# Attention stage of a streaming encoder: first loads ahead of the gates' weights, key stores on GpSimd, two tile pools, sample rows in two runs, cache keys in a value buffer

## The chip, the core and the metric

The kernel runs on one core of a Trainium2 chip. A core has five engines with a queue of instructions each: TensorE (PE, matrix products; its weight loads are shown as PEld), VectorE (DVE), ScalarE (ACT), GpSimd (POOL) and SyncE (SP), which here only issues transfers (DMAs). ACT and POOL issue transfers too. The metric is the device time in microseconds of one execution; the time given for a kernel is the median of its runs.

## The reference

One layer of a trunk, for a prompt of 2048 frames and a sample of 32 new frames, at model width 1024. After a normalisation and modulation by a condition vector, one input projection feeds two branches. Branch A is attention with 8 heads of 64, in chunks of 64 frames: each chunk sees itself and the 8 chunks before it, and the sample sees 512 cached rows and its own 32. Branch B is a gated linear recurrence. Sigmoid gates merge both, an output projection follows, and then a gated MLP with a convolution of width 3. For the attention of the sample:

```python
kk = jnp.concatenate([k_cache, k_new], axis=1)
vv = jnp.concatenate([v_cache, v_new], axis=1)
s = jnp.einsum('bqhd,bkhd->bhqk', q, kk).astype(jnp.float32) * (d ** -0.5) + bias
p = jax.nn.softmax(s, axis=-1).astype(vv.dtype)
o = jnp.einsum('bhqk,bkhd->bqhd', p, vv)
```

Everything is fp32. Products are made of high and low parts (`h`, `l` at the end of a name): a value is rounded by ACT to its high part, DVE subtracts for the low part, and PE makes two or three passes.

## The kernel before, in words

All 2080 columns (prompt and sample) stand transposed, in blocks of 416. The program has these stretches: preparation and the first input projections (to about 480 us); the recurrence of branch B, in chunks, with the projections to attention queries and keys (`qk_stream`) between its steps; the attention stage (from about 767 to 1486 us); then the merge and the MLP.

**Stores before the attention.** `t_evac` (L197) takes a block of a projection out of PSUM. For queries and keys it splits the block into a high part `qh` (ACT) and a low part `ql` (DVE) and stores both to DRAM (`qs`, `ks`): the high one by ACT's queue, the low one by SP's (L209 to L211), in two transfers of 64 rows each. The last chunk of the stream is the keys of heads 6 and 7 (`k`, c = 3), in five blocks. For the newest keys ACT also stores plain rows (`kr`, L216). The state of the recurrence is stored by POOL (`state_io`, L779).

**The attention stage** has 72 units: 8 heads by 9, where g = 0 to 7 are 256 query rows of the prompt each (two row blocks) and g = 8 is the 32 sample rows. A unit (L937) goes in steps: its loads (bias `nb` and the keys and values of chunk 0 in unit 0; queries `q2`; every second unit 512 more keys and values), its scores and softmax for the two row blocks, and then, for each block of 128 keys, a transpose of the probabilities `P` on PE, a copy out of PSUM and products with the values into `py`. The softmax goes through four engines: PE writes scores to `F` (far) and `PN` (near), DVE adds the bias and takes maxima into `mx`, ACT takes the exponentials (L927, L930), and POOL scales `P` by the reciprocal of the sum (L934).

Between these steps PE works through `filler`: the projections to the 2048 gate columns (16 chunks of 128 columns, five blocks of 416 each, eight slices of three passes: L78 to L80), whose weights come in pieces `wr` (L185) that ACT and DVE split into `wh` and `wl`, and then a projection of branch B. The loop from L1185 on sets how many filler steps stand between the steps of a unit and when the next unit's scores and the loads of the one after it come. Ahead of the loop stand the first loads, 16 steps of filler, and the first scores (L1173 to L1175). PE's order is this written order; in the attention stage a scheduler orders the other engines.

For the sample (g = 8, L995 to L1010) there are five blocks of keys: four of the cache, one of the new keys. For each block PE makes one transpose into a PSUM tile of its own, DVE copies it to `pt`, and PE makes one product with 64 value columns (L993), two blocks later; after each of the first steps a filler step may stand. The cached keys come as `ck` (L862), in a buffer of the ring of `P`, and are split into the key buffers by a deferred function (`LATE`).

Transfers issued by SP and ACT in the attention stage run over eight lanes that both queues share: before a transfer is issued, the one before it in its lane has to have landed. This is in the waits of the built program.

Of the kernel before, what the change touches and what calls it, by code (L numbers as in the profile page):

```python
# [21 lines left out]
TP, TS = 2048, 32  # L22
# [36 lines left out]
def encoder_step(ctx: ExitStack, tc: tile.TileContext, I, O):  # L59
# [116 lines left out]
    psm = pool(mix, "psm", bufs=2, space=PSUM)  # L176

    def w_pieces(wp, c0, n, w, kp, wr=2):

        hi = wp.tile([128, KD, w], F32R, name="wh", tag="wh")  # L180
        lo = wp.tile([128, KD, w], F32R, name="wl", tag="wl")

        def piece(kk):
            raw = wp.tile([128, kp, w], F32, name="wr", tag="wr", bufs=wr)
            nc.sync.dma_start(raw[:, :, :n], dap(w_in, kk * 128 * WIN + c0, [[WIN, 128], [128 * WIN, kp], [1, n]]))  # L185
            nc.scalar.activation(hi[:, kk:kk + kp, :n], raw[:, :, :n], AF.Copy)
            nc.vector.tensor_sub(lo[:, kk:kk + kp, :n], raw[:, :, :n], f32(hi[:, kk:kk + kp, :n]))

        return (hi, lo), [lambda kk=kk: piece(kk) for kk in range(0, KD, kp)]
# [7 lines left out]
    def t_evac(stg, kind, c, b, p):  # L197

        cols = slice(NB * b, NB * b + NB)
        if kind in "qk":  # L200
# [7 lines left out]
            dst = qs if kind == "q" else ks  # L208
            for x, r0, q_ in ((qh, 0, nc.scalar), (ql, 64, nc.sync)):  # L209
                for j in range(2):  # L210
                    q_.dma_start(dst[2 * c + j, r0:r0 + 64, cols], f32(x[64 * j:64 * j + 64]))  # L211
# [621 lines left out]
    with ExitStack() as st:  # L833
        stg = pool(st, "stgT", bufs=3)
        att_st = st.enter_context(ExitStack())
        at_ = pool(att_st, "att")
        psN = pool(att_st, "psN", space=PSUM)
# [10 lines left out]
        def load_chunk(h, c):  # L848
# [12 lines left out]
            if c == 5:  # L861
                ck = at_.tile([128, 512], F32, name="ck", tag="P", bufs=4)  # L862
                for r in (0, 64):
# [3 lines left out]
            else:  # L867
# [5 lines left out]
                else:  # L873
                    nc.sync.dma_start(vr, dap(vn, 512 * c * NCOL + 128 * pair, [[NCOL, 128], [128 * NCOL, 4], [1, 128]]))
            KH[c], KL[c] = kh, kl
            vr = vr[:, :, 64 * j:64 * j + 64]
            vs = None
            if c < 4:
# [6 lines left out]
                LATE.append(values)  # L885
            V[c] = (vr, vs)

# [5 lines left out]
        def scores(h, i, q2, qc, keys, PN):  # L893
# [20 lines left out]
            assert a == tot  # L914
            mx = at_.tile([128, 8], F32, name="mx", tag="mx", bufs=4)
            P = at_.tile([128, 640], F32, name="P", tag="P", bufs=4)
            nr = P[:m, far:tot]
# [19 lines left out]
        def unit(h, g):  # L937
# [57 lines left out]
            if g == 8:  # L995
                for x, kt in enumerate(steps):
                    first, last = x == 0, x == len(steps) - 1
                    pp_ = psP.tile([128, 2, 128], F32, name="pp", tag="pP")
                    kn = 128 if kt < 4 else TS
                    nc.tensor.transpose(pp_[:kn, 0, :TS], P[:TS, 128 * kt:128 * kt + kn], ident[:TS, :TS])  # L1000
                    pt = at_.tile([128, 128], F32, name="pt", tag="pt", bufs=3)
                    nc.vector.tensor_copy(pt[:kn, :TS], pp_[:kn, 0, :TS])
                    todo.append((py[0:64, :TS], vt[kt], pt[:kn, :TS], first, last))
                    if len(todo) > 2:
                        pv(1)
                    yield 1
                while len(todo) > 1:
                    pv(1)
                    yield 1
                pv(1)  # L1010
            else:
# [38 lines left out]
            if g == 8:  # L1050
                nc.vector.tensor_copy(ya[:, :TS], py[0:64, :TS])
                nc.sync.dma_start(yaT[64 * h:64 * h + 64, TP:T], ya[:, :TS])
# [119 lines left out]

        ustep(us[0])  # L1173
        pull(filler, 16)
        ustep(us[0])  # L1175
# [1155 lines left out]
```

## Time and profile before

| what | value |
|---|---|
| median of 3 runs | 3178.28 us (3174.66 to 3178.77) |
| the profiled execution | 3174.99 us, with a span of 3173.3 us |
| mean granted PE clock | 0.992 |
| PE busy | 3056.5 us, 96% of the span |
| DVE, ACT, POOL busy | 2243.6, 1649.5, 263.7 us |
| PE's longest idle time at the start of the attention | 5.86 us, ending at 782.46 |

In the rows of a timeline the first number is the start in us from the span's begin, the second the length in us; then come engine, line, operation, output and inputs with partitions x elements; `xN` means N instructions in a row; in brackets stands the idle time ahead of it and what ended it. `SPq` and `ACTq` rows are the issue of transfers by those queues. In a row of grouped instructions three times are minimum, median and maximum in ns. The granted clock is the share of full speed that PE got.

### The profile page before, as it was taken

The page shows a single profiled execution, that of the slowest core. Times are in us where ns is not written, and L with a number is a line of the kernel's source. Part 1 is how long each engine was busy: PE and PEld are TensorE (multiplying, and loading weights), DVE is VectorE, ACT ScalarE, POOL GpSimd, SP SyncE. Part 2 cuts the span into 40 slices and gives each one's busy share as a digit, 9 for nine tenths or more (in the row PEclk, how much of TensorE's full clock was granted, in tenths as well). Part 3 has the DMA queues.
Part 4 walks back from the last instruction along what each step waited for, and adds up shares of the span by engine and source line. Part 5 has one row for each costly group of instructions (what it writes and reads, how often), then busy time and mean ns, then how long its engine had stood idle before and what let it go on. Part 6 is the DMA issues. An engine that isn't in the chain of part 4 may idle for free. (4 is left out here: it accounts for less than half of the span.)

```text
span 3173.3 us, 56451 instructions
## 1 busy us (share of the span) xinstructions
PE 3056.5 (96%) x19748; PEld 2942.5 (93%) x19748; DVE 2243.6 (71%) x4903; ACT 1649.5 (52%) x3792; POOL 263.7 (8%) x417
## 2 busy tenths in 40 slices
PE   6999999999999999999999999999999999999997
PEld 4899999998999999988999899999999999999997
DVE  6735617774555545566577799998888778897877
ACT  4412224443554545544454655567656556576755
POOL 3201201111111111111000000000000000000001
PEclk9999999999999999999999999999999999999998
DMA  7344435554433333576457686787887667888784
GB/s 226 101 141 127 143 98 143 132 134 132 119 103 110 99 105 117 164 224 194 129 176 223 211 260 208 224 258 227 248 262 218 189 189 231 263 252 280 239 266 148
DMA packets 598799, 580.13 MB, mean 183 GB/s; under 512 B 53201, under 2 KB 527010, under 8 KB 598514
## 3 DMA queue, kind: packets, MB, share of 16 engines
q1 hardware_dynamic: 553826, 528.92, 55.6%
q10 hardware_dynamic: 44432, 47.34, 4.6%
q8 instruction: 155, 2.54, 0.3%
q14 instruction: 130, 1.06, 0.1%
q0 software_dynamic: 256, 0.26, 0.0%
HBM read 388.71 MB, written 187.65 MB: 182 GB/s over the span
## 5 line engine op out<-in xcount | busy, mean ns | idle before, releaser
L1876 PE MATMUL ad<-hA,hB 128*128 128x350 f32 (+2 forms) x1734 | 300.8, 323 | 5.3 <-DVE hB L1818 2.7
L78 PE MATMUL pm<-hA,wh 128*128 128x416 f32 x768 | 290.3, 378 | 0.0
L1876 PEld LDWEIGHTS ad<-hA,hB 128*128 128x128 f32 x1734 | 281.7, 189 | 7.3 <-ACT work L2002 3.8
L79 PE MATMUL pm<-hA,wh 128*128 128x416 f32 x768 | 269.9, 351 | 0.0
L80 PE MATMUL pm<-hA,wl 128*128 128x416 f32 x768 | 269.9, 351 | 0.0
L1818 DVE TENSOR_TENSOR hA<-raws,hA 128x512 fp32r<-128x512 f32 (+1 forms) x367 | 242.0, 668 | 12.5 <-ACT hA L1813 12.2
L1813 ACT ACTIVATE hA<-raws 128x512 fp32r<-128x512 f32 (+1 forms) x367 | 222.0, 617 | 31.7 <-DMA raws<-in_w_up_dram 10.8
L1876 PE MATMUL ad<-hA,hA 128*128 128x348 f32 (+2 forms) x1308 | 226.9, 324 | 3.0 <-ACT work L2002 2.2
L1876 PE MATMUL g<-hA,hB 128*128 128x348 f32 (+2 forms) x1248 | 217.2, 323 | 6.7 <-ACT work L1998 3.9
L1876 PEld LDWEIGHTS ad<-hA,hA 128*128 128x128 f32 x1308 | 213.1, 190 | 4.3 <-ACT work L2002 2.8
L1876 PEld LDWEIGHTS g<-hA,hB 128*128 128x128 f32 x1248 | 202.4, 188 | 9.4 <-ACT work L1998 5.0
L1876 PE MATMUL ad<-hA 128*128 128x350 f32 (+2 forms) x1173 | 204.9, 324 | 4.2 <-DVE hA L1728 4.1
L1876 PEld LDWEIGHTS ad<-hA 128*128 128x128 f32 x1173 | 191.5, 190 | 5.0 <-DVE hA L1728 4.4
L1818 DVE TENSOR_TENSOR hB<-raws,hB 128x512 fp32r<-128x512 f32 (+1 forms) x289 | 191.0, 668 | 6.7 <-ACT hB L1813 6.3
L1813 ACT ACTIVATE hB<-raws 128x512 fp32r<-128x512 f32 (+1 forms) x289 | 175.9, 617 | 26.5 <-DMA raws<-in_w_up_dram 11.6
L69 ACT ACTIVATE pth<-pp 128x256 fp32r<-128x256 f32 (+1 forms) x288 | 106.0, 374 | 145.1 <-PE pp L1023 137.8
L78 PE MATMUL pn<-wh,hA 128*128 128x256 f32 (+1 forms) x624 | 177.8, 285 | 0.0
L79 PE MATMUL pn<-wl,hA 128*128 128x256 f32 (+1 forms) x624 | 177.1, 284 | 0.0
L80 PE MATMUL pn<-wh,hA 128*128 128x256 f32 (+1 forms) x624 | 177.0, 284 | 0.0
L1985 ACT COPY g<-ad 128x348 f32<-128x348 f32 (+2 forms) x102 | 44.3, 434 | 243.1 <-PE ad L1876 155.9
L72 DVE TENSOR_TENSOR ptl<-pp,pth 128x256 fp32r<-128x256 f32 (+1 forms) x288 | 117.5, 413 | 63.6 <-ACT pth L69 61.0
L1876 PE MATMUL g<-hA,hA 128*128 128x350 f32 (+2 forms) x894 | 156.1, 323 | 3.3 <-ACT g L1985 1.7
(505 smaller groups left out, 8470.0 us busy)
## 6 DMA issues: line engine op xcount, KB each, us to landing
raws<-in_w_up_dram SPq DMA_DIRECT2D x220, 256.0 KB, 4.3
raws<-sW SPq DMA_DIRECT2D x176, 256.0 KB, 3.7
sW<-raws SPq DMA_DIRECT2D x88, 256.0 KB, 3.5
raws<-in_w_down_dram SPq DMA_DIRECT2D x80, 256.0 KB, 4.8
wr<-in_w_in_dram SPq DMA_DIRECT2D x76, 256.0 KB, 3.2
sgT<-tx ACTq DMA_DIRECT2D x80, 208.0 KB, 2.7
wa<-in_w_ada_dram SPq DMA_DIRECT2D x64, 256.0 KB, 3.0
keys<-ks SPq DMA_DIRECT2D x128, 128.0 KB, 2.8
```

What stands on the lines that cost most here:

```text
L69: i = nc.scalar.activation(hi, src, AF.Copy)
L72: nc.vector.tensor_sub(lo, src, f32(hi))
L78: nc.tensor.matmul(out, ah, bh, start=first and i == 0, stop=False)
L79: nc.tensor.matmul(out, ah, bl, start=False, stop=False)
L80: nc.tensor.matmul(out, al, bh, start=False, stop=last and i == n - 1)
L1813: act = nc.scalar.activation(hi[:, :n], raw(i, n), AF.Copy)
L1818: nc.vector.tensor_sub(lo[:, :n], raw(i, n), f32(hi[:, :n]))
L1876: nc.tensor.matmul(out[:, :w], l_[:, k], r_[:, k, :w], start=first and k == 0 and i == 0, stop=k == n - 1 and i == 2, skip_group_check=True)
L1985: nc.scalar.copy(g[:, 0, :w], ad[:, 0, :w])
```

## The change

It has these parts.

1. A flag makes the first piece of gate weights that is asked for after the first loads keep its place in the program's order on SP, so that the loads written ahead of it stand ahead of it.
2. The low halves of the last chunk of keys (c = 3) are stored by POOL's queue and no longer by SP's.
3. `mx` and `P` have a pool of their own, `atP`, opened ahead of the other attention pool. By this the attention tiles lie over other tiles of the stages before: the bias buffer is now free with the last state product of the recurrence, the first key buffer with the last state store and state update.
4. `ck` stands in the ring of the values (`vr`, three buffers) and no longer in that of `P`.
5. For the sample the five transposes stand in one run and go to one PSUM tile; DVE copies it in two pieces; two yields follow; then the five products stand in one run. The weights of a product are 128 value columns, both heads of a pair, and the result is taken from the 64 rows of the head in question.

The diff:

```diff
@@ -175,6 +175,8 @@
     mix = ctx.enter_context(ExitStack())
     psm = pool(mix, "psm", bufs=2, space=PSUM)

+    behind = [False]
+
     def w_pieces(wp, c0, n, w, kp, wr=2):

         hi = wp.tile([128, KD, w], F32R, name="wh", tag="wh")
@@ -182,7 +184,10 @@

         def piece(kk):
             raw = wp.tile([128, kp, w], F32, name="wr", tag="wr", bufs=wr)
-            nc.sync.dma_start(raw[:, :, :n], dap(w_in, kk * 128 * WIN + c0, [[WIN, 128], [128 * WIN, kp], [1, n]]))
+            d = nc.sync.dma_start(raw[:, :, :n], dap(w_in, kk * 128 * WIN + c0, [[WIN, 128], [128 * WIN, kp], [1, n]]))
+            if behind.pop():
+                tc.keep_in_program_order(d)
+            behind.append(False)
             nc.scalar.activation(hi[:, kk:kk + kp, :n], raw[:, :, :n], AF.Copy)
             nc.vector.tensor_sub(lo[:, kk:kk + kp, :n], raw[:, :, :n], f32(hi[:, kk:kk + kp, :n]))

@@ -206,7 +211,7 @@
             else:
                 split(qh, ql, p)
             dst = qs if kind == "q" else ks
-            for x, r0, q_ in ((qh, 0, nc.scalar), (ql, 64, nc.sync)):
+            for x, r0, q_ in ((qh, 0, nc.scalar), (ql, 64, nc.gpsimd if kind == "k" and c == 3 else nc.sync)):
                 for j in range(2):
                     q_.dma_start(dst[2 * c + j, r0:r0 + 64, cols], f32(x[64 * j:64 * j + 64]))
             a = max(NB * b, TP - 512)
@@ -833,6 +838,7 @@
     with ExitStack() as st:
         stg = pool(st, "stgT", bufs=3)
         att_st = st.enter_context(ExitStack())
+        atP = pool(att_st, "attP")
         at_ = pool(att_st, "att")
         psN = pool(att_st, "psN", space=PSUM)
         psF = pool(att_st, "psF", bufs=2, space=PSUM)
@@ -859,7 +865,7 @@
                 kh, kl = KHL[0][:, a:a + 512], KHL[1][:, a:a + 512]
                 vr = at_.tile([128, 4, 128], F32, name="vr", tag="vr", bufs=KB)
             if c == 5:
-                ck = at_.tile([128, 512], F32, name="ck", tag="P", bufs=4)
+                ck = at_.tile([128, 512], F32, name="ck", tag="vr", bufs=KB)
                 for r in (0, 64):
                     nc.sync.dma_start(ck[r:r + 64], dap(I["cache_kT"], h * 64 * 512, [[512, 64], [1, 512]]))
                 LATE.append(lambda: split(kh, kl, ck))
@@ -873,6 +879,7 @@
                 else:
                     nc.sync.dma_start(vr, dap(vn, 512 * c * NCOL + 128 * pair, [[NCOL, 128], [128 * NCOL, 4], [1, 128]]))
             KH[c], KL[c] = kh, kl
+            pair_v = vr
             vr = vr[:, :, 64 * j:64 * j + 64]
             vs = None
             if c < 4:
@@ -883,7 +890,7 @@
                     nc.gpsimd.tensor_sub(vs[:, :, 1, :], vr, f32(vs[:, :, 0, :]))

                 LATE.append(values)
-            V[c] = (vr, vs)
+            V[c] = (pair_v if c > 3 else vr, vs)

         def load_bias(h):
             nb = at_.tile([128, 256], F32, name="nb", tag="nb", bufs=2)
@@ -912,8 +919,8 @@
                     a += e
                     c0 += e
             assert a == tot
-            mx = at_.tile([128, 8], F32, name="mx", tag="mx", bufs=4)
-            P = at_.tile([128, 640], F32, name="P", tag="P", bufs=4)
+            mx = atP.tile([128, 8], F32, name="mx", tag="mx", bufs=4)
+            P = atP.tile([128, 640], F32, name="P", tag="P", bufs=4)
             nr = P[:m, far:tot]
             nc.vector.tensor_tensor_reduce(nr, N[:m, :near], nb[:m, bj:bj + near], 1.0, -3e38,
                                            op0=OP.add, op1=OP.max, accum_out=mx[:m, 0:1])
@@ -993,21 +1000,18 @@
                         nc.tensor.matmul(o_, l_, r_, start=f_, stop=e_, skip_group_check=True)

             if g == 8:
-                for x, kt in enumerate(steps):
-                    first, last = x == 0, x == len(steps) - 1
-                    pp_ = psP.tile([128, 2, 128], F32, name="pp", tag="pP")
+                pp_ = psP.tile([128, 2, 128], F32, name="pp", tag="pP").rearrange("p a b -> p (a b)")
+                pt = at_.tile([128, 5 * TS], F32, name="pt", tag="pt")
+                for kt in steps:
                     kn = 128 if kt < 4 else TS
-                    nc.tensor.transpose(pp_[:kn, 0, :TS], P[:TS, 128 * kt:128 * kt + kn], ident[:TS, :TS])
-                    pt = at_.tile([128, 128], F32, name="pt", tag="pt", bufs=3)
-                    nc.vector.tensor_copy(pt[:kn, :TS], pp_[:kn, 0, :TS])
-                    todo.append((py[0:64, :TS], vt[kt], pt[:kn, :TS], first, last))
-                    if len(todo) > 2:
-                        pv(1)
-                    yield 1
-                while len(todo) > 1:
-                    pv(1)
-                    yield 1
-                pv(1)
+                    nc.tensor.transpose(pp_[:kn, TS * kt:TS * kt + TS], P[:TS, 128 * kt:128 * kt + kn], ident[:TS, :TS])
+                nc.vector.tensor_copy(pt[:, :4 * TS], pp_[:, :4 * TS])
+                nc.vector.tensor_copy(pt[:TS, 4 * TS:], pp_[:TS, 4 * TS:5 * TS])
+                yield 1
+                yield 1
+                for kt in steps:
+                    kn = 128 if kt < 4 else TS
+                    nc.tensor.matmul(py[:, :TS], vt[kt], pt[:kn, TS * kt:TS * kt + TS], start=kt == 0, stop=kt == 4)
             else:

                 def values(kt_):
@@ -1048,7 +1052,8 @@
                         yield 1
             ya = at_.tile([64, 256], F32, name="ya", tag="ya", bufs=2)
             if g == 8:
-                nc.vector.tensor_copy(ya[:, :TS], py[0:64, :TS])
+                r = 64 * (h % 2)
+                nc.vector.tensor_copy(ya[:, :TS], py[r:r + 64, :TS])
                 nc.sync.dma_start(yaT[64 * h:64 * h + 64, TP:T], ya[:, :TS])
             else:
                 yh = at_.tile([64, 256], F32, name="yh", tag="yh")
@@ -1171,6 +1176,7 @@
                 next(u)

         ustep(us[0])
+        behind[0] = True
         pull(filler, 16)
         ustep(us[0])
         pull(filler, 4)
```

SP's queue from the last stores of queries to the second key loads of head 0 (`qs` and `ks` are stores of the query and key halves, `wr` gate weights, `nb` the bias, `keys`, `vr` and `q` the loads of a unit). Before:

```order
L211 DMA qs<-ql 64x416 x2
L185 DMA wr<-in_w_in_dram 128x4x128 x2
L211 DMA ks<-ql 64x416 x8
L185 DMA wr<-in_w_in_dram 128x4x128
L211 DMA ks<-ql 64x416 x2
L185 DMA wr<-in_w_in_dram 128x4x128
L890 DMA nb<-nbD 128x256
L870 DMA keys_8746<-ks 64x512 x2
L870 DMA keys_8747<-ks 64x512 x2
L874 DMA vr<-vn 128x4x128
L959 DMA q_8757<-qs 128x256
```

With the change:

```order
L216 DMA qs<-ql 64x416 x2
L897 DMA nb<-nbD 128x256
L876 DMA keys_8749<-ks 64x512 x2
L876 DMA keys_8750<-ks 64x512 x2
L880 DMA vr<-vn 128x4x128
L966 DMA q_8760<-qs 128x256
L187 DMA wr<-in_w_in_dram 128x4x128 x2
```

The ten stores of keys have left SP, the bias, the first keys, values and queries stand ahead of the gate weights. On POOL the stores stand between those of the recurrence's state:

```order
L216 DMA ks<-ql 64x416 x2
L784 DMA out_gla_prompt_dram<-SBP_4962 64x128 x2
L691 TENSOR_TENSOR kd<-qk,E 128x32
L784 DMA out_gla_prompt_dram<-SBP_4966 64x128 x2
L691 TENSOR_TENSOR kd<-qk,E 128x32
L216 DMA ks<-ql 64x416 x4
L784 DMA out_gla_sample_dram<-SBS_4964 64x128 x2
L216 DMA ks<-ql 64x416 x2
L784 DMA out_gla_sample_dram<-SBS_4968 64x128 x2
L216 DMA ks<-ql 64x416 x2
```

Six of them now stand ahead of the first state store of the sample, eight ahead of the second one, and two behind both.

PE at the sample unit of head 0 (`pm` rows are gate projections, `PN` scores of the next head, `pp` the transposes, `py` the products). Before, two of the five blocks:

```order
L1000 MATMUL pp<-ident,P 128x32
L993 MATMUL py<-pt,vr 64x32
L78 MATMUL pm<-hB_676,wh 128x416
L79 MATMUL pm<-hB_677,wh 128x416
L80 MATMUL pm<-hB_676,wl 128x416
L910 MATMUL PN<-keys_8746,q_9859 128x256
L911 MATMUL PN<-keys_8747,q_9859 128x256
L78 MATMUL pm<-hB_676,wh 128x416
L79 MATMUL pm<-hB_677,wh 128x416
L80 MATMUL pm<-hB_676,wl 128x416
L1000 MATMUL pp<-ident,P 128x32
L993 MATMUL py<-pt,vr 64x32
```

With the change:

```order
L1007 MATMUL pp<-ident,P 128x32 x4
L1007 MATMUL pp<-ident,P 32x32
L78 MATMUL pm<-hA_104,wh 128x416
...
L917 MATMUL PN<-keys_8749,q_9862 128x128
L918 MATMUL PN<-keys_8750,q_9862 128x128
L78 MATMUL pm<-hB_676,wh 128x416
L79 MATMUL pm<-hB_677,wh 128x416
L80 MATMUL pm<-hB_676,wl 128x416
L1014 MATMUL py<-pt,vr 128x32 x4
L1014 MATMUL py<-pt,vr_9742 128x32
```

Five transposes and five products now each stand together, with twelve passes of the projection and a score between them. The products are 128 columns wide where they were 64.

ACT at the split of head 0's cached keys. Before, it stands between the last transposed blocks of unit 7 and the exponentials of the sample (32 rows):

```order
L1055 COPY yh<-py 64x256
L69 ACTIVATE keys_8746<-ck 128x512
L69 ACTIVATE pth<-pp 128x256 x2
L222 ACTIVATE tx<-pm 128x416
L927 ACTIVATE P,mx<-P,mx 32x160
```

With the change it stands in unit 5, between two rounds of transposed blocks and the exponentials of the first of its two row blocks:

```order
L1060 COPY yh<-py 64x256
L69 ACTIVATE pth<-pp 128x256 x3
L69 ACTIVATE keys_8749<-ck 128x512
L934 ACTIVATE P,mx<-P,mx 128x256
L937 ACTIVATE P,mx<-F,mx 128x384
```

DVE's half of the split stands likewise ahead of the maximum of the second row block of unit 5. Both halves write the key buffer of chunk 1, which the scores of that unit's second block are the last to read in part.

## The prediction

> **What bounds the kernel now.** I read the page's busy shares first, then the tensor engine's (PE's) timeline around the start of the attention stage, then the queue that feeds it there.
>
> ```profile
> PE 3056.5 (96%) x19748; PEld 2942.5 (93%) x19748; DVE 2243.6 (71%) x4903; ACT 1649.5 (52%) x3792; POOL 263.7 (8%) x417
> ```
>
> PE is busy for 96% of the time, and its order is fixed by hand, so only two things can move the end: PE passes that become fewer or cheaper, and places where PE stands. The longest stand in the attention stage is at its door:
>
> ```profile
> 775.29 0.35 PE L78 MATMUL pm<-hA,wh 128*128 128x416 f32 x1
> ...
> 776.24 0.35 PE L80 MATMUL pm<-hA,wl 128*128 128x416 f32 x1
> 782.46 0.47 PE L910 MATMUL PN<-keys,q 128*128 128x128 f32 x1 [5.86 <-DMA keys<-ks]
> ...
> 785.77 0.35 PE L80 MATMUL pm<-hA,wl 128*128 128x416 f32 x1
> ```
>
> ```profile
> 776.30:782.50 6.20, 0.34 (x3) 0.04 (x1) 0.00 (x0) 0.93 (x2) 0.16 (x1) 0.71 0.90 269
> 782.50:786.50 4.00, 4.00 (x14) 3.88 (x15) 0.62 (x4) 0.49 (x2) 0.94 (x2) 0.60 0.40 110
> ```
>
> Projection steps follow each other every 0.19 us (775.29 to 776.24 is five steps). At 776.24 the first score of head 0 finds no keys and PE stands 5.86 us; the second table (PE busy, weight loads, DVE, ACT, POOL, granted clock, DMA share) shows the clock granted after it at 0.60, and the steps come slower until 785.77. From 776.24 to 785.77 are 9.53 us. Eight later projection steps and the step at 776.24 itself would take 9 x 0.19 = 1.7 us, and the two score passes some 0.3 more: 2.0. So about **7.5 us** are lost at this door, 5.9 of them idle and 1.6 in the slow stretch.
>
> Why the keys are late stands in the SP queue's timeline:
>
> ```profile
> 750.96 11.87 SPq L211 DMA_DIRECT2D ks<-ql  x6
> 768.17 0.37 SPq L185 DMA_DIRECT2D wr<-in_w_in_dram  x1
> ...
> 772.74 0.37 SPq L185 DMA_DIRECT2D wr<-in_w_in_dram  x1
> 773.28 0.38 SPq L890 DMA_DIRECT2D nb<-nbD  x1
> 773.89 2.40 SPq L870 DMA_DIRECT2D keys<-ks  x4
> ...
> 776.97 1.48 SPq L959 DMA_DIRECT2D q<-qs  x3
> ```
>
> Nothing of head 0 is issued before 773.28, because its loads stand behind two gate-weight pieces (issued at 768.17 and 772.74) and behind the last stores of keys. The queries leave SP at 776.97 at the earliest, after PE has come.
>
> **The change, part A: the first loads.** The reordered SP queue has the bias, four key loads, the values and the queries ahead of all pieces of gate chunk 1, and ten key stores have gone to POOL. What holds them next is not SP. The changed tiles lie over tiles of the recurrence, so the first key load waits for POOL's last state store, and the second half of the keys, the values and the queries each wait for the DMA before them in their lane, of which the last is ACT's store of key rows.
>
> ```profile
> 762.93 1.03 POOL L779 DMA_DIRECT2D out_gla_sample_dram<-SBS  x2 [2.52 <-DVE SBS L748]
> ```
>
> ```profile
> 770.80 0.51 ACTq L216 DMA_DIRECT2D out_k_aT_dram<-kr  x1
> ```
>
> ```profile
> DMA to landing us min/median/max: 1.9/2.8/5.3
> ```
>
> The last line is of the loads and stores of the score keys: from issue to landing. POOL's last store ends its issue at 763.96; with the six key stores now ahead of or between the state stores, at about half a microsecond each as the two state stores here (1.03 for two), it may end some 1 to 2 us later, and it lands by 768. The queries wait for the store issued at 770.80; with a landing of 1.9 to 2.8 they go out at 773 to 774, and land 1.9 to 2.8 later still: 775 to 777. PE comes at 776.24. So a stand of 0 to 1 us is likely, and with the 5.3 landing for the last of them up to 774 + 5.3 - 776.24 = 3.1. Lower end of the gain: 7.5 less 3.1 and 0.4 of slower clock, so -4; upper end -7.5. I take **-6**, as the middle of the landings would leave a stand near 0.5 and I allow as much again for the slower clock. The weights that are pushed back are those of gate chunk 1. The program pulls 16 of chunk 0's 40 steps (five blocks, eight slices, three passes a step) before the first score, so 24 steps, 72 passes of 0.19, 13.7 us of PE work at least, cover them; without that cover they would cost a landing, 2.8, and the split of a piece behind it.
>
> **Part B: the sample's transposes and products in runs.** For each head, PE leaves its projection stream seven times for the 32 sample rows:
>
> ```profile
> 866.28 0.35 PE L80 MATMUL pm<-hA,wl 128*128 128x416 f32 x1
> 866.56 0.24 PE L1000 MATMUL pp<-ident,P 32*128 32x32 f32 x1
> ...
> 867.03 0.35 PE L79 MATMUL pm<-hA,wh 128*128 128x416 f32 x1
> ...
> 869.52 0.34 PE L80 MATMUL pm<-hB,wl 128*128 128x416 f32 x1
> ...
> 869.97 0.30 PE L993 MATMUL py<-pt,vr 128*64 128x32 f32 x2
> ...
> 870.49 0.35 PE L79 MATMUL pm<-hB,wh 128*128 128x416 f32 x1
> ...
> 875.46 0.34 PE L80 MATMUL pm<-hA,wl 128*128 128x416 f32 x1
> ...
> 876.26 0.35 PE L79 MATMUL pm<-hA,wh 128*128 128x416 f32 x1
> ```
>
> Each pair of ends holds two projection steps, 0.38 us. A lone transpose costs 867.03 - 866.28 - 0.38 = 0.37 (of which the pass is a small part: the rest is the switch away and back). A transpose with a product costs 870.49 - 869.52 - 0.38 = 0.59, a lone product (two passes) 876.26 - 875.46 - 0.38 = 0.42. A head has two, three and two of them: 2 x 0.37 + 3 x 0.59 + 2 x 0.42 = 3.35 us.
>
> What a run costs is shown by the recurrence's own transposes of the same shape, and by passes with weights of the full 128 columns:
>
> ```profile
> 766.59 0.35 PE L80 MATMUL pm<-hA,wl 128*128 128x416 f32 x1
> 766.87 0.43 PE L768 MATMUL pty<-ident,y 32*128 32x32 f32 x4
> ...
> 767.53 0.35 PE L79 MATMUL pm<-hA,wh 128*128 128x416 f32 x1
> ```
>
> ```profile
> 733.91 0.60 PE L768 MATMUL pty<-ident,y 128*128 128x128 f32 x4
> 734.34 0.60 PE L715 MATMUL pa<-qbd,kd 128*128 128x256 f32 x2
> ```
>
> Four transposes in a run cost 767.53 - 766.59 - 0.38 = 0.56, so one more costs (0.56 - 0.37) / 3 = 0.063, and five cost 0.62. Of five products the first costs 0.42 and the other eight passes between 0.063 (32 columns streamed) and (734.34 - 733.91) / 4 = 0.108 (128 streamed) each: 0.92 to 1.28. A head then costs 1.54 to 1.90 and saves 1.45 to 1.81: over eight heads -11.6 to -14.5. The new passes stream 32 columns, so I go nearer to the first row, at 0.08 a pass: **-13.4**. The two copies between the runs stand where two yields give PE projection work to do, and DVE has three copies fewer, so I take them as hidden; PE orders are otherwise alike.
>
> In the Trainium skill, the page TensorE: Matmul & The Clock Gate, section LDWEIGHTS (loading the stationary operand), has the time of a weight load go by its columns, about P / 1.2 ns, whatever the rows. By that each of the ten passes pays 53 ns more for 128 columns than for 64, an estimate of 0.53 us a head or 4.3 in all, and B would be -9.1. The full-width row above, at 0.108 with four times the streamed columns, leaves less room for it.
>
> **Part C: the cache keys.** They are split into two parts by ACT and DVE before the sample's scores:
>
> ```profile
> L69 ACT ACTIVATE keys<-ck x8: 629/631/632, 857.5 to 1461.1; 128x512 fp32r<-128x512 f32 x8
> L72 DVE TENSOR_TENSOR keys<-ck,keys x8: 691/692/694, 858.2 to 1461.8; 128x512 fp32r<-128x512 f32 x8
> ...
>   PE F L910: 1.7, 3
>   PE F L911: 1.5, 4
> ```
>
> Their lateness costs PE 1.7 + 1.5 = 3.2 us now. With the raw keys in a value buffer they arrive a good way earlier, and the split moves into the middle of unit 5, ahead of the softmax of its rows. That softmax has no slack:
>
> ```profile
> 828.24 0.80 POOL L934 TENSOR_SCALAR P<-P,mx 128x640 f32<-128x640 f32 x1 [1.15 <-ACT tx L222]
> ```
>
> ```profile
> 829.05 0.38 PE L1023 MATMUL pp<-ident,P 128*128 128x128 f32 x2
> ...
> 830.62 0.34 PE L910 MATMUL F<-keys,q 128*128 128x384 f32 x1
> ...
> 832.11 0.33 PE L910 MATMUL F<-keys,q 128*128 128x384 f32 x1
> ```
>
> POOL's scaling of a unit's probabilities ends at 829.04 and PE's first transpose of them starts at 829.05. What delays the chain of ACT, DVE and POOL delays PE. The split overwrites the key buffer that unit 5's second score block still reads, so ACT holds its queue, with the exponentials of the first block behind it, until that score (1.49 us after the first, 830.62 to 832.11), then takes 0.63; DVE holds the second block's maximum for 0.69. The same two softmaxes in ACT's timeline:
>
> ```profile
> 832.77 0.51 ACT L927 ACTIVATE P<-P,mx 128x256 f32<-128x256 f32 x1 [0.20 <-DVE mx L924]
> ...
> 835.16 0.51 ACT L927 ACTIVATE P<-P,mx 128x256 f32<-128x256 f32 x1
> ...
> 836.12 0.20 ACT L930 ACTIVATION_READ_ACCUMULATOR P<-F,mx 128x1 f32 x1
> ```
>
> The first block's exponentials start at 832.77, 0.66 after the second score came, so the hold for that score is hidden and most of the 0.63 too. The bounds are nothing and all 1.32 us of the two splits a head; I take 0.5, nearer the lower one for that reason, since only DVE's 0.69 is likely to show: +4.0, less the 3.2 that go, so **+1** (from -3.2 to 10.6 - 3.2 = +7.4).
>
> **Sum.** -6 - 13.4 + 1 = -18.4 against the profiled execution's 3174.99 gives 3156.6. The runs' median, 3178.28, is 3.3 above that execution; as I do not know on which of them the new runs will lie, I add half of it: **3158**. Its own range, from the bounds of the three terms taken together without all extremes at once, is 3150 to 3165.
>
> **Rivals.**
>
> *The first loads stay late (chance 0.14).* Key stores and state stores now share POOL's queue. If its DMAs wait for their turn and the last state store comes 8 us later than at 763.96, the first key load goes out at 772 plus a landing, no sooner than before (773.89), and A shrinks to -1: 3174.99 - 1 - 13.4 + 1 + 1.6 = 3163. For it: the page shows POOL nearly idle but says nothing of how ten stores go there in a row. Against it: two state stores needed 1.03 us.
>
> The Trainium skill, page SBUF — State Buffer, section SBUF: two separate sides, warns of this: a DMA issued on the GpSimd queue has its descriptors written by GpSimd, which is locked out while DVE runs some of its two-port copies. By it the ten stores could be held by DVE's copies; the two stores in the row above show no such hold.
>
> *The products do not get cheaper in a run (0.08).* With weights twice as wide each product may still cost the 0.42 of a lone one: 5 x 0.42 + 0.62 = 2.72 a head, B = -5.0, and the time 3174.99 - 6 - 5.0 + 1 + 1.6 = 3166.6. Against it: four full-width passes in a run above need 0.43 together.
>
> *The split lands on the softmax chain, and the kernel is slower (0.07).* If ACT's wait for the second score and both splits come in series with the chain, and the second block's exponentials queue behind the first's, then unit 5 of each head is late by 1.49 + 0.63 + 0.69 and by one block of exponentials, 836.32 - 835.16 = 1.16. The sum is 3.97 a head, 31.8 in all, less the 3.2: C = +28.6, and 3174.99 - 6 - 13.4 + 28.6 + 1.6 = 3185.8. It decides from about 2.8 us a head, where it eats up A and B. For it: POOL's scaling ends as PE comes. Against it: the 0.66 us of ACT above, in which the hold ends before its cost begins.
>
> *Small gains only (0.09).* A at its lower end, B at -11.6 and C at +7.4 or somewhat above: -4 - 11.6 + 7.4 = -8.2, so 3168.
>
> **How the numbers follow.** The forecast holds 0.62, the rivals 0.14, 0.08, 0.07 and 0.09. The time is 3158. The range goes down to 3149 and up to 3169, so as to take in the late loads, the dear products and the small gains; the slower case stays out. About 0.2%, 6.4 us, is what a measurement here can tell from no change: faster means below 3171.9. The forecast and the late loads lie clear of it; of the dear products and the small gains about a third could slip into it. So faster 0.84, same 0.09, slower 0.07.
>
> **What would show it.** A: the stand ahead of the first score below 2 us and the clock there near 1.00, with the queries issued near 773; a stand above 4 says that POOL or a lane is the hold. B: one run of five transposes and one of ten product passes a head, 0.6 and 0.9 to 1.3 us beyond the projection steps; a stand ahead of the products says that the copies aren't hidden. C: no wait of the sample's scores for the split, and at unit 5 of each head PE's wait for POOL's scaling at or below 0.5 us. The forecast is wrong if the waits for POOL grow by more than 10 us over the stage, or if the attention stage shrinks by less than 10 us.

## The result and the profile after

The changed kernel takes 3162.56 us (median of 6 runs, 3159.37 to 3164.47) against 3178.12 us before: a ratio of 0.9950, with a 95% interval of 0.9940 to 0.9961. Measured again later on the same chip as two other versions it took 3163.38 us against 3177.30 (0.9954, 0.9942 to 0.9967). The forecast was 3158, with a range of 3149 to 3169.

The profiled execution has a span of 3160.3 us, 13.0 less than before. The page's first row shows that PE did slightly less and is still the bound:

```profile
PE 3047.7 (96%) x19748; PEld 2947.7 (93%) x19748; DVE 2239.8 (71%) x4879; ACT 1648.8 (52%) x3792; POOL 269.4 (9%) x427
```

To see where the 13.0 us lie, both traces are cut at the same instructions of PE: at the last transposes of the recurrence (L768 before), at the scores of head 0's second row block, and at the first step behind the attention stage (`px`). The first stretch is called the door here, the second the stage. A row gives the stretch, its length, the busy time of PE, its weight loads, DVE, ACT and POOL, then PE's granted clock, DMA share and GB/s. Before:

```profile
766.87:786.53 19.66, 13.80 (x67) 13.18 (x67) 2.50 (x7) 5.48 (x11) 1.10 (x2) 0.83 0.66 184
786.53:1486.22 699.69, 686.24 (x4267) 633.09 (x4267) 390.49 (x1388) 353.31 (x1043) 126.15 (x169) 1.00 0.45 134
```

After:

```profile
769.50:783.27 13.77, 12.29 (x67) 11.79 (x67) 1.95 (x7) 5.45 (x11) 1.93 (x4) 1.00 0.73 206
783.27:1475.02 691.75, 676.17 (x4268) 637.35 (x4267) 387.23 (x1365) 353.38 (x1043) 126.74 (x170) 1.00 0.47 138
```

The door is 5.89 us shorter and the stage 7.94. The door begins 2.63 us later than before (769.50 against 766.87), though SP issues the same transfers in the same order up to there in both, and DVE's rows are already 2.5 us apart at the 56th us; and what is behind the stage is 1.80 shorter. 2.63 - 5.89 - 7.94 - 1.80 is -13.0. The traces of the experiments below have the door begin anywhere from 765.73 to 769.50, so the 2.63 is how one execution differs from another, and stretches tell more here than spans.

At the door, PE's timeline and SP's of the changed kernel:

```profile
778.87 0.35 PE L80 MATMUL pm<-hA,wl 128*128 128x416 f32 x1
780.70 0.33 PE L917 MATMUL PN<-keys,q 128*128 128x128 f32 x1 [1.48 <-DMA q<-qs]
```

```profile
764.92 0.35 SPq L897 DMA_DIRECT2D nb<-nbD  x1
769.00 6.53 SPq L876 DMA_DIRECT2D keys<-ks  x4
776.00 0.38 SPq L880 DMA_DIRECT2D vr<-vn  x1
776.42 0.68 SPq L966 DMA_DIRECT2D q<-qs  x1
```

The stand is 1.48 us instead of 5.86 and the clock stays at 1.00. The bias and the first key loads go out before PE comes, but the four key loads take 6.53 us to issue, and the queries are last. What SP waited for in this stretch (us in total, times, longest):

```profile
SPq L876 <- DMA out_gla_sample_dram<-SBS: 3.3, 1, 3.3
SPq L876 <- DMA ks<-qh: 4.3, 1, 4.3
SPq L880 <- DMA ybT<-yt: 0.5, 1, 0.5
```

The first key load waited for POOL's state store. The second half of the keys then waited 4.3 us for a store of ACT's (`ks<-qh`, key rows of heads 6 and 7, which head 0 doesn't read), and the values 0.5 us for another. The queries followed with no wait of their own.

The waits of PE in the stage, before and after (engine, instruction, what it waited for: us in total, times, longest). Before:

```profile
PE pp L1023 <- POOL P L934: 3.6, 7, 0.8
PE PN L910 <- DVE mx L918: 1.9, 3, 1.0
PE F L910 <- ACT keys L69: 1.7, 3, 0.7
PE px L78 <- DVE tg L1151: 0.8, 1, 0.8
PE pp L1023 <- DVE ptl L72: 0.7, 2, 0.4
```

After:

```profile
PE pp L1027 <- POOL P L941: 4.5, 9, 0.8
PE PN L917 <- DVE mx L925: 2.9, 4, 1.0
PE px L78 <- DVE tg L1156: 2.6, 1, 2.6
PE pp L1027 <- DVE ptl L72: 2.2, 7, 0.3
```

The waits for the split of the cached keys are gone. In their place PE waits more for POOL, for low halves (`ptl`) in seven heads where it was two, and 2.6 us for a gated row (`tg`) at the stage's end, where it was 0.8.

### The profile page after: what moved, and what is told of

Read it like the earlier page. It is cut to its first block, busy times and chain, and to the rows that moved or that the text cites. A ratio compares the mean times of both kernels' runs of the same rounds, so it can differ in the third digit from the quotient of the medians.

```text
span 3160.3 us, 56426 instructions
## 1 busy us (share of the span) xinstructions
PE 3047.7 (96%) x19748; PEld 2947.7 (93%) x19748; DVE 2239.8 (71%) x4879; ACT 1648.8 (52%) x3792; POOL 269.4 (9%) x427
## 3 DMA queue, kind: packets, MB, share of 16 engines
q14 instruction: 129, 1.06, 0.1%
```

## The experiments

Door and stage of every run, read as above. For the stand the first score's idle time is given. The kernel before was run beside each group again, with medians of 3177.30 to 3179.28, and each ratio is to the runs of its own group. What follows the stage takes from 1684.6 to 1691.3 us in these traces, with no edit there; so a difference of a few us is read from door and stage, and the medians only bear it out.

| kernel | median, us | ratio to before, 95% interval | stand | door | stage |
|---|---|---|---|---|---|
| before | 3178.12 | | 5.86 | 19.66 | 699.69 |
| the change | 3162.56 | 0.9950 (0.9940 to 0.9961) | 1.48 | 13.77 | 691.75 |
| the change again | 3163.38 | 0.9954 (0.9942 to 0.9967) | 0.23 | 12.54 | 694.89 |
| loads, stores, pools alone | 3173.66 | 0.9981 (0.9971 to 0.9991) | none | 12.26 | 702.26 |
| sample runs alone | 3168.13 | 0.9960 (0.9948 to 0.9973) | 5.7 | 20.14 | 692.00 |
| cached keys alone | 3177.53 | 0.9992 (0.9983 to 1.0001) | 4.6 | 18.47 | 698.93 |
| change, stores on SP | 3161.81 | 0.9943 (0.9929 to 0.9956) | 1.61 | 13.90 | 691.55 |
| change, weights not kept back | 3162.20 | 0.9944 (0.9930 to 0.9957) | 2.33 | 16.00 | 690.78 |
| change, one pool | 3164.66 | 0.9952 (0.9938 to 0.9965) | 2.68 | 14.99 | 689.71 |
| change, 64 value columns | 3159.76 | 0.9931 (0.9918 to 0.9943) | none | 12.40 | 687.47 |
| change, late sample scores | 3159.18 | 0.9941 (0.9928 to 0.9955) | 0.61 | 12.91 | 688.61 |
| change, both of these | 3157.47 | 0.9934 (0.9922 to 0.9947) | 0.87 | 13.19 | 687.93 |
| and queries first | 3158.80 | 0.9943 (0.9929 to 0.9956) | none | 12.05 | 685.90 |

### Each part alone

The first three experiments put one part of the change each on the kernel before. The first takes parts 1 to 3; the diff is against the changed kernel, beside its sample unit, which is that of before:

```diff
-                ck = at_.tile([128, 512], F32, name="ck", tag="vr", bufs=KB)
+                ck = atP.tile([128, 512], F32, name="ck", tag="P", bufs=4)
...
-            V[c] = (pair_v if c > 3 else vr, vs)
+            V[c] = (vr, vs)
```

> The change without its sample runs and with the cached keys back in the ring of P: only the order of the first loads, the key stores on GpSimd and the pool of its own for P and mx. Theory (the two traces): PE's stand at the first score is 1.5 us instead of 5.9, no slow clock follows, and from the last projection step before it to the steps after it 5.8 us are won; the rest of the attention stage is as in the kernel before, with 3.2 us of waits for the split of the cached keys. Time about 5.8 us below before. Rival: part of the 5.8 us comes from the other edits, or the displaced gate weights cost something later; then the stage behind the first score is longer than before by a microsecond or more.

The time is 5.5 us below before (3173.66 against 3179.16 in that comparison). The door is 7.4 us shorter, with no stand at all, so the theory holds there. But the stage is 2.6 us longer than before, which is the sign that was named for the rival. Of that, 1.6 stand in the waits for the cached keys, which are loaded as late as before:

```profile
PE F L916 <- ACT keys L69: 3.2, 3, 1.6
```

ACT's own wait for that transfer is 10.0 us over eight heads here, and 8.6 before. That the loads' new order causes this isn't shown; one execution against one can't tell it from chance.

The second is the kernel before with the sample's runs (the diff is the one for g == 8 above):

> The kernel before with only the sample's transposes and products in two runs. Theory: the stand at the first score stays at 5.9 us and the waits for the split cached keys at 3.2 us; a head's transposes and products cost 0.59 + 1.35 us beyond the projection steps instead of 3.35, so 1.4 us a head and 11.3 us in all are won. No new waits of PE for the low halves in unit 7. Rival: the waits of 0.3 us for the low halves of the transposed probabilities in unit 7, which the changed kernel shows in seven heads, come with the runs; then the gain is 8 us.

The median is 11.0 us below before, with an interval from 8.6 to 16.5, and there is no new wait for the low halves. The stage is 7.7 us shorter. The waits for the cached keys are 0.8 us longer, and a wait that was 0.77 before has grown at its end:

```profile
PE px L78 <- DVE tg L1150: 3.0, 1, 3.0
```

So 11.3 of saved PE time show as 7.7: 2.2 went into the wait at the end and 0.8 into the keys; 0.6 I can't place.

The third moves only the cached keys' buffer:

```diff
-                ck = at_.tile([128, 512], F32, name="ck", tag="P", bufs=4)
+                ck = at_.tile([128, 512], F32, name="ck", tag="vr", bufs=KB)
```

> The kernel before with only the cached keys in a value buffer. Theory: the waits of the sample's scores for the split (3.2 us) go, but the sample's maxima and exponentials now stand ahead of the low halves of unit 7 on DVE, and PE waits for those 0.46 us in each of seven heads (3.2 us), and 0.9 us in unit 5 of head 0: in all 0 to +1 us against before, no difference that can be measured. Rival (the prediction's): the split delays unit 5 of every head by 0.5 us, and unit 7 shows no new waits; +1 us in all too, so the two are told apart by the places of the waits.

The time is 1.6 us below, within the interval no difference. The waits for the split are gone from the list, and the seven waits for low halves are there, without the runs:

```profile
PE pp L1023 <- DVE ptl L72: 2.2, 7, 0.3
```

They belong to this part. In unit 5 PE has new waits for POOL in heads 0, 5 and 7 alone (0.45, 0.18 and 0.30 us); in head 0 a gate weight is split at the same place. In the other heads the list has no new wait there.

The three parts alone add to -18.1 us (5.5, 11.0 and 1.6). The change itself has -15.6 and -13.9. The intervals reach 3 to 4 us to either side of each, so this difference can't be told from none.

### Which part opened the door

Each of the next three takes one thing back from the changed kernel: the stores on SP, the weights not kept behind, one pool for all tiles.

```diff
-            for x, r0, q_ in ((qh, 0, nc.scalar), (ql, 64, nc.gpsimd if kind == "k" and c == 3 else nc.sync)):
+            for x, r0, q_ in ((qh, 0, nc.scalar), (ql, 64, nc.sync)):
```

> The changed kernel with the last key stores issued by SP again, all ten ahead of the first loads; all else as in the change. Theory L (lanes and the tiles underneath hold the loads in the changed kernel, which sent its queries at 776.4): SP's last store goes out near 771 to 772, four keys, values and queries follow in 3.6 us, so the queries leave near 776 too and PE's stand at the first score is 1 to 2.5 us, the door as in the change within 1 us. Theory S (the stores on SP were what held the loads in the kernel before): the stand is 4 us or more.

The door is 13.90 us, as in the change within what two executions of the change differ by (12.54 and 13.77). SP's timeline of this kernel:

```profile
769.12 0.54 SPq L897 DMA_DIRECT2D nb<-nbD  x1
770.01 2.38 SPq L876 DMA_DIRECT2D keys<-ks  x4
772.44 0.59 SPq L880 DMA_DIRECT2D vr<-vn  x1
773.07 0.63 SPq L966 DMA_DIRECT2D q<-qs  x1
```

All loads go out later than with the stores on POOL, but in one go, and the queries leave 7.2 us after the door begins at 765.88, against 6.9 in the change. Theory L holds: in the change the wait of the second half of the keys had held the queries for as long.

```diff
         ustep(us[0])
-        behind[0] = True
         pull(filler, 16)
```

> The changed kernel without the flag that keeps the gate weights behind the first loads: three weight pieces stand ahead of the bias again, and only the third waits for a split. Theory: in the kernel before that third piece went out at 768.17 and only the fourth, at 772.74, was late; so the first loads are hardly held and the stand at the first score stays at 0 to 2 us, the door as in the change within 1 us. Rival: the weights ahead of the loads were the main hold; then the stand is 4 us or more and the time 4 us above the changed kernel's.

The stand is 2.33 us, between the theory and its rival, and the door 16.00. The third weight piece left at 769.26 and the bias after it, so weights ahead do cost something. More than the stand, it is the clock behind it:

```profile
780.00:784.00 4.00, 3.98 (x15) 3.85 (x16) 0.62 (x4) 0.50 (x3) 1.10 (x2) 0.62 0.89 242
```

15 passes in 4 us at a granted clock of 0.62.

```diff
-            P = atP.tile([128, 640], F32, name="P", tag="P", bufs=4)
+            P = at_.tile([128, 640], F32, name="P", tag="P", bufs=4)
```

and the same for `mx`; the pool of its own goes.

> The changed kernel with P and mx in the common pool again, so that the first keys lie over the buffers of the last key stores' low halves and wait until POOL's last store has landed. Theory: that store ends its issue near 772 and lands near 774, the keys leave then and the queries near 777 to 778, so the stand at the first score is 3 to 5 us, 2 to 4 us of the gain at the door are lost. Rival: the lanes hold the queries as long in any case and the stand stays below 2 us.

The keys go out at 772.66, by the profile after a wait for ACT's store of the key rows (`kr`) and not, as the theory had it, for POOL's last store; the queries go out at 775.73; the stand is 2.68 us, just below the 3 to 5 expected, with the clock at 1.00 behind it:

```profile
779.00:783.00 4.00, 3.96 (x23) 3.94 (x24) 1.87 (x7) 1.75 (x5) 1.12 (x2) 1.00 1.06 304
```

No one of the three parts carries the door: without any one of them the stand is 1.6 to 2.7 us, with all 0 to 1.5, and with none 4.6 to 5.9. None of the three times can be told from the change's. What a part would do alone, without the other two, was not run.

### What a product in the run costs

```diff
-                    nc.tensor.matmul(py[:, :TS], vt[kt], pt[:kn, TS * kt:TS * kt + TS], start=kt == 0, stop=kt == 4)
+                    nc.tensor.matmul(py[0:64, :TS], vt[kt], pt[:kn, TS * kt:TS * kt + TS], start=kt == 0, stop=kt == 4)
```

with `vt` the 64 columns of the head and the result read from rows 0 to 63.

> The changed kernel with products 64 value columns wide, one head's, instead of 128; all else as in the change. Theory: a pass of the product run costs 0.12 us because the weights of 128 columns take 192 ns to load, against 133 ns for 64 columns; with 64 columns the ten passes cost 0.06 to 0.08 us each, the run 0.9 to 1.1 instead of 1.35, and the kernel gets 2 to 4 us faster than the changed one. Rival: the cost of a pass has nothing to do with the columns of its weights; then the run stays at 1.35 us and the time is the changed kernel's.

Head 0's sample unit in PE's timeline, in the change:

```profile
862.85 0.35 PE L80 MATMUL pm<-hA,wl 128*128 128x416 f32 x1
863.14 0.46 PE L1007 MATMUL pp<-ident,P 32*128 32x32 f32 x5
...
863.82 0.35 PE L79 MATMUL pm<-hA,wh 128*128 128x416 f32 x1
...
865.94 0.35 PE L80 MATMUL pm<-hB,wl 128*128 128x416 f32 x1
866.13 1.31 PE L1014 MATMUL py<-pt,vr 128*128 128x32 f32 x10
...
867.67 0.35 PE L79 MATMUL pm<-hB,wh 128*128 128x416 f32 x1
```

and with 64 columns:

```profile
860.77 0.35 PE L80 MATMUL pm<-hB,wl 128*128 128x416 f32 x1
861.05 0.88 PE L1013 MATMUL py<-pt,vr 128*64 128x32 f32 x10
...
862.15 0.35 PE L79 MATMUL pm<-hB,wh 128*128 128x416 f32 x1
```

Less the two projection steps of 0.38, the transposes cost 0.59, the wide products 867.67 - 865.94 - 0.38 = 1.35 and the narrow ones 862.15 - 860.77 - 0.38 = 1.00. The weight loads (minimum, median, maximum in ns) of the change, then of the narrow version:

```profile
L1014 PEld LDWEIGHTS py<-pt,vr x80: 181/192/192, 865.9 to 1462.3; 128*128 128x128 f32 x64, 32*128 32x128 f32 x16
```

```profile
L1013 PEld LDWEIGHTS py<-pt,vr x80: 128/138/138, 861.0 to 1453.6; 128*64 128x64 f32 x64, 32*64 32x64 f32 x16
```

A wide load takes 54 ns more. Over ten passes the run is 0.35 us dearer, 2.8 us in eight heads; the stage is 4.3 shorter, 1.4 of them by shorter waits (0.7 for the gated row at its end, 0.7 for maxima). The median is 2.8 us below the changed kernel's, but measured in another comparison and with overlapping intervals: the gain is shown by the runs' length.

### Where the waits for low halves come from

DVE's timeline of the change in unit 7 of head 1:

```profile
940.38 0.20 DVE L931 TENSOR_SCALAR mx<-mx 32x1 f32<-32x1 f32 x1
941.79 0.15 DVE L938 TENSOR_TENSOR mx<-mx 32x1 f32<-32x1 f32 x1 [1.20 <-ACT P L937]
941.97 0.15 DVE L940 RECIPROCAL mx<-mx 32x1 f32<-32x1 f32 x1
942.05 0.42 DVE L72 TENSOR_TENSOR ptl<-pp,pth 128x256 fp32r<-128x256 f32 x1
```

DVE stands 1.20 us for ACT's exponentials of the sample, with a low half of unit 7 queued behind. In the kernel before, the split of the cached keys held the sample's scores, and the halves went first. Moving the sample's scores one step later puts another half ahead:

```diff
                 late()
+                yield 0
                 PN = psN.tile([128, 2, 256], F32, name="PN", tag="PN")
                 P = scores(h, 16, q2, 0, keys, PN)
                 yield 0
-                yield 0
```

> The changed kernel with the sample's scores one step later in the order, at 0.45 of unit 7 instead of 0.3. Theory: the waits of PE for the low halves in unit 7 (0.3 us in each of seven heads, 0.46 us of lost time each, 3.2 in all) come from the sample's maxima and sums, for which DVE waits on ACT ahead of those halves; with the scores later one fewer half stands behind them, these waits go or shrink, and the time is 1 to 3 us below the changed kernel's. Rival: the chain only meets other halves, or the sample's probabilities then come late for its transposes; then nothing is won.

PE's waits for low halves ahead of transposes are no longer in the list, and the stage is 3.1 us shorter (688.61 against 691.75), the 3.2 of the theory. The wait at the stage's end is 3.3 us here, and the median is 3.4 us below the changed kernel's, in separate comparisons whose intervals overlap.

### Both gains, and the queries first

The last three ran on one chip, with the change again beside two further versions.

> The changed kernel itself, on the chip of the two versions beside it, to compare with them. Both theories: 15 us below the kernel before; PE's stand at the first score 0.2 to 2 us.

The stage is 3.1 us longer than in the first trace of the same kernel. Beside the waits shown above it has one for gated rows in the middle of branch B's steps:

```profile
PE pm L78 <- DVE tg L1156: 3.0, 2, 2.1
```

The other version has both edits, the narrow products and the late scores:

> The changed kernel with products of 64 value columns and with the sample's scores one step later. Theory: both gains add, since the one is PE work and the other a wait in another unit: the stretch from the second block's scores to the first gated step after the attention takes 688 - 3 = 685 us (687.5 with narrow products alone, 688.6 with late scores alone, 691.8 in the change), and the time is 5 to 7 us below the changed kernel's. Rival: both run into the same wait at the stage's end (gate rows for the last steps of branch B, 2.6 us in the change); then it stays at 687 to 688.

The time is 3157.47 us, 5.9 below the change on the same chip, as expected, though the two intervals overlap; the stage is 7.0 shorter. Its stage of 687.93 us holds 2.3 of that same wait for gated rows, without which it would be at the 685 to 686 expected.

```diff
             c = g // 2
             q2 = at_.tile([128, 256], F32R, name="q2", tag="q2", bufs=3)
+            if g == 0:
+                nc.sync.dma_start(f32(q2), qs[h, :, 0:256])
+                load_chunk(h, 0)
+                load_bias(h)
```

in place of the three loads of the first unit of a head.

> As before, and in the first unit of a head the queries are loaded ahead of the keys, and the bias behind the values. Theory: at the door the queries were the last to come, held by the lane of ACT's store of key rows; now they go out as soon as the tiles are free, near 762 to 766, and the keys' second half is last, about 0.5 to 1 us sooner than the queries were: the stand at the first score is below 0.7 us. Rival: the keys then wait as long and nothing is won, or the bias, now last, holds the softmax of the first block, and the stretch behind the door gets longer.

The door is the shortest of all, 12.05 us, with PE busy throughout:

```profile
765.77:777.82 12.05, 12.05 (x68) 11.88 (x68) 1.21 (x5) 4.79 (x11) 1.82 (x4) 1.00 0.77 219
```

The queries left at 761.19. DVE then waits for the bias, but PE doesn't. In the median (3158.80) nothing of this shows; the 0.87 us of stand that could be won are less than the runs scatter by.

## Why the prediction was right, and where not

**The door (A, forecast -6, bounds -4 and -7.5).** Right in size, and in its mechanism up to the hold that ended last. The profiled execution has -5.89, the second one -7.12. The queries were indeed last. They left at 776.42, where 773 to 774 was worked out, but the whole execution was 2.6 us later there: counted from the begin of the door it is 6.9 us, against 6.1 to 7.1 forecast. The hold was another than the one named: not ACT's store of key rows ahead of the queries, but the store of ACT's that the second half of the keys waited 4.3 us for. That the number fits so well is in part luck. The terms of the prediction, 7.5 less 0.5 of stand and 0.5 of slower clock, give 6.5 and not the 6 that it took; the stand came out at 1.48 and the slower clock at nothing, which gives 6.0.

That POOL's queue would hold the first loads, the first rival, is refuted. Its stores issue at half a microsecond each (1.03 to 1.28 for two), the last state store ends its issue 2.8 us ahead of the door, as before (2.9), and moving the stores back to SP changes the door by nothing that can be seen. The prediction costed the three edits as one, and the runs give them no prices of their own: taking one back lengthens the door by 0.1 to 2.2 us, so any two of them open most of it.

**The runs (B, forecast -13.4, bounds -11.6 to -14.5).** The mechanism is right, the size was off at one term. The five transposes cost 0.59 us, 0.62 forecast. The ten product passes cost 1.35 and not the 1.06 taken or the 0.92 to 1.28 of the bounds: a pass beyond the first two cost (1.35 - 0.42) / 8 = 0.116 us, where 0.08 was taken. The step that failed is the choice of the nearer row: I went by the streamed columns, towards the 0.063 of a 32-column transpose. The other row, 0.108 with the same 128 columns of weights and four times as many streamed, was the nearer one, and with 64 columns of weights a pass costs (1.00 - 0.42) / 8 = 0.073. So a head saves 3.35 - 0.59 - 1.35 = 1.41, and eight save 11.3. The rival of dear products (2.1 us a head) is refuted too.

The rule of the Trainium skill's page TensorE: Matmul & The Clock Gate, section LDWEIGHTS (loading the stationary operand), to which the prediction gave little room, agrees with the traces in the difference and not in the times. By it a load takes about 107 ns for 128 columns and 53 ns for 64, so 53 ns lie between them; the traces have 192 and 138 ns, 54 apart. The 4.3 us in eight heads worked out from it, an estimate, compare with 2.8 measured in the runs' length, 0.043 us a pass; why it is less than the loads differ by isn't shown.

What I did not see at all is that a gain of PE inside the stage can end in a wait at its end. The last gated rows are made by DVE from loaded rows of gates (`tg<-sgT`). Two rows of DVE, the last one before and the last but one in the change:

```profile
1485.49 0.59 DVE L1151 SCALAR_TENSOR_TENSOR tg<-tg,pm 128x416 f32<-128x416 f32 x1 [1.08 <-PE pm L80]
1472.16 0.59 DVE L1156 SCALAR_TENSOR_TENSOR tg<-tg,pm 128x416 f32<-128x416 f32 x1 [2.02 <-DMA tg<-sgT]
```

Before, DVE waited for PE there; now it waits for the transfer. PE stands 2.6 us in the change and 3.0 with the runs alone, against 0.77 before. About 1.8 of the 11.3 are given back there.

**The cached keys (C, forecast +1, bounds -3.2 and +7.4).** The sum came out near nothing, as forecast, but by luck, since the mechanism is wrong. Alone, this part measured 1.6 us below before, with an interval from 5.4 below to 0.3 above, so that the +1 lies just outside. The waits of 3.2 us went, as said. The step that failed is the 0.5 us of delay in unit 5 of every head: PE has new waits there in heads 0 and 7 alone (0.75 and 0.29 us, for POOL), and in both ACT splits a weight between the exponentials of the two row blocks besides. The 0.66 us of room that the prediction read from ACT's timeline are those of head 0, where the wait did come; what covers the split in the other heads wasn't measured. The cost stands in unit 7 instead, in the place that was left: without the split in front of them, the sample's maxima come sooner, and DVE waits for their exponentials ahead of the low halves. I looked at what the moved step would delay, and not at what it had held back. With it falls the slower rival, a serial split in unit 5.

**The sum.** -5.9 for the door, -11.3 for the runs, -3.2 for the keys; given back: 0.46 us in each of the five heads that had no wait for a low half before (2.3), 0.9 in unit 5 of heads 0 and 7, some 1.0 at one score that waits for maxima, 1.8 at the end. That is -14.4 against -13.8 of door and stage in the trace. The measured median, 15.6 below, is 4.6 above the forecast's 3158 and inside its range. Some 1.5 of this lie in the base: 3174.99 and half of 3.3 are that much below the median before. The effect itself falls 2.8 short of the 18.4; the product passes (2.1) and the stage's end (1.8) would make 3.9, and what is between is less than the runs scatter by.

**Open.** Whether the parts together give less than the 18.1 us of the three alone, the intervals can't settle. And the waits for gated rows in the middle of branch B's steps, 3.0 us in one execution of the change and none in another, come with waits of DVE for transfers; what makes these late was not tried.

## What to carry to other kernels

A step that is moved away may have held something back, which then comes sooner and meets other work: look at what follows the gap it leaves as well as at where it lands. When small matrix products are put in a run, look at the columns of their weights before those that are streamed: with 32 columns streamed, a pass cost 0.116 us here with 128 columns of weights and 0.073 with 64. And where several edits free the same load, taking one back can show little; cost them together, by what is last at the end.

## What was unexpected of the hardware

PE's clock after a short stand does not follow from the stand's length alone. At the door a stand of 2.33 us was followed by 4 us at a granted clock of 0.62 (weights not kept back), and one of 2.68 us by none below 1.00 (one pool). The first cost 16.00 - 12.05 - 2.33 = 1.6 us beyond the stand itself, as much as the 5.86 us of the kernel before. At the stage's end, where PE stands for the last gated row, it is the same. These are the 4 us behind a stand of 3.25 us (late sample scores) and behind one of 3.00 us (one pool):

```profile
1468.42:1472.42 4.00, 4.00 (x33) 4.00 (x34) 0.83 (x2) 0.00 (x0) 0.00 (x0) 1.00 0.99 328
1471.34:1475.34 4.00, 4.00 (x18) 4.00 (x19) 0.00 (x0) 0.00 (x0) 0.00 (x0) 0.50 0.99 321
```

The longer stand was followed by the full clock and the shorter by half of it. A stand of 2.73 us there was followed by 0.57 in one kernel (the change again) and by 1.00 in another (both edits). What decides isn't shown.
